# A hybrid decoder layer on one Trainium2 core: the second head's loads issued from ScalarE, and the first two pairs of channel blocks of the up projection interleaved

## The chip, the core and the metric

The kernel runs on one core of one Trainium2 chip. The metric is the device time of one execution in microseconds, lower is better. The engines are named as in the profile: PE (TensorE, matmuls; PEld its weight loads), DVE (VectorE), ACT (ScalarE), POOL (GpSimd) and SP (SyncE, which here issues DMAs). Each engine works its own instructions in program order; between engines there are semaphores.

## What is computed

One decoder layer over 2048 tokens with 1024 channels in float32: a mixer of three head groups (forgetting attention, mLSTM, HGRN2), and a gated feed-forward part with a causal convolution of three taps. Cut to what matters here:

```python
def _fox_attention(q, k, v, c):            # 8 heads of 64, causal, with forget gates c
    ...
        s = jnp.einsum('bhqd,bhkd->bhqk', qi, k) * scale
        s = s + ci[..., None] - c[:, :, None, :]
        ...
        p = jax.nn.softmax(s, axis=-1)
        return jnp.einsum('bhqk,bhkd->bhqd', p, v)

def _conv_glu(h, w_up, conv_w, conv_b, w_down):
    u = _causal_dwconv(h @ w_up, conv_w) + conv_b
    gate, up = jnp.split(u, 2, axis=-1)
    return (jax.nn.silu(gate) * up) @ w_down

def reference(x, ...):
    for l in range(DEPTH):                 # DEPTH = 1, D_MODEL = 1024, D_FF = 2816
        h = _rms(x, norm_mix_g[l])
        x = x + _mixer(h, ...)
        h = _rms(x, norm_ffn_g[l])
        x = x + _conv_glu(h, w_up[l], ffn_conv_w[l], ffn_conv_b[l], w_down[l])
    return x
```

## The kernel before

**Stages.** The input projection and the other mixers run to about 905 us of the profiled span, the attention from there to about 1378, the output projection to about 1585. Then comes the feed-forward part in two halves of 1024 tokens: up projection of half 0 to about 2017, down projection of half 0, then both again for half 1. Float32 products are made of three matmuls of operands split in a high and a low half (names with h and l, or w tiles in pairs): high by high, low by high, high by low.

**Attention** (`attention`, with its order written by hand). A head has four blocks of 512 queries, and a block `qb` has 4·qb + 4 steps `j` of 128 keys. A step makes scores `s` on PE (L936, L937, and a mask at L939), then on ACT the exponential `pf` (L943) and its high half `ph` (L945), then the low half `pl` on POOL or DVE (L949). Three steps later (SKEW) the products with V follow on PE (L962 to L964). The score tile in PSUM has two buffers. Between the scores PE also makes products for the row maxima of later blocks (L886), which DVE reduces; every finished block adds an `oT` on ACT (L970). A head's operands QA, KA, QB, KB and V lie in two sets of buffers, for even and odd heads, and come by ten DMAs (`att_load`, L851), all issued by SP. The second head's are called for in step 6 of the first head, right behind that step's scores; those of the other heads in the third step of the head before.

**Feed-forward, up** (`ffn_up`). The order of instructions here isn't written by hand: a scheduler with estimates of its own sets it when the kernel is built. The 22 pairs of channel blocks (`p`, a gate block and an up block each) are taken in the order 0, 11, 1, 12 and so on; each `p` is called a pair below: pair 1, pair 2 and so on in that order. For a pair the product of h and w_up is made by a Winograd scheme of seven block products rather than eight: b11, t4, b21, t2, t1, t3 and b22, each of 12 matmuls of 128x512 (L1339), named by the operand from h. The other operands are blocks of w_up or sums of them: a11, s2, a12, s1, s3, a22, s4 (`up_blocks`): four loads on SP (L1302), four sums on DVE (L1313), seven high halves on ACT (L1307) and as many low halves on POOL (L1308). For pair 1, a11, a12 and a22 are made early (`up_first`, L1288). The results lie in two PSUM tiles of 1024 columns (g and u), of four such tiles in all, so pair 3 writes the tiles of pair 1. DVE adds up partial results (L1383, L1389, L1390, L1393, L1395), then come the convolution (ACT L1353, DVE L1354 and L1355, and a halo on ACT, L1357), the gate (ACT L1398) and the product (DVE L1400). After every second pair the result's blocks and their sums are stored (`g_blocks`, ACT's DMAs, L1421 and L1428), and in half 0 the same is done for the weights of the down projection (`w_blocks`: SP's loads L1438, POOL's differences L1441, ACT's stores L1442).

The high and low halves of two of the operands from h, t3 and b22, don't exist before the output projection's buffers are free; they are made when the up projection of half 0 begins (`h_parts` with `h_split`: ACT L1227; DVE or POOL L1228; sums L1246).

## Time and profile before

| what | value |
|---|---|
| time, median of 3 runs | 2878.68 us (2875.48, 2878.68, 2880.37) |
| the profiled execution: its time | 2879.12 us |
| the profiled execution: its span | 2877.0 us |
| mean granted TensorE clock | 0.982 of full speed |
| matmuls, PE busy | 15053, 2788.7 us |
| DMA | 411.06 MB, 143 GB/s in the mean |

In the rows of the profile shown below, a timeline's row has the start in us from the span's start, the duration, the engine, the line, the operation, the tiles written and read and a count; in brackets stands idle time of the engine just before it, and what ended it. SPq and ACTq are the issues of DMAs, as the sequencer of SP or ACT spends time on them. A row of the chain of waits has the start, the duration and what the end of the program was waiting for then.

### The profile page before, as it was taken

To read this page: it belongs to the slowest core of one execution; us is meant where nothing else is said; L and a number is where in the kernel's file an instruction comes from. 1 tells how busy PE (TensorE), PEld (TensorE's weight loads), DVE (VectorE), ACT (ScalarE), POOL (GpSimd) and SP (SyncE) were. 2 spreads that over 40 slices of the span, in tenths; PEclk is the share of its full clock that TensorE was granted. 3 is DMA by queue.
4 is the path that set the end of the run, shared out by engine and by line. 5 is a ranking of instruction groups with operands and counts; after the bars stand their busy time and mean duration, and the time that the engine had idled before them with its cause. 6 is when DMAs were issued, how large, how long until landed. Compare 5 with 4: busy or idle time off the path is not lost. (4 is left out here: it accounts for less than half of the span.)

```text
span 2877.0 us, 42992 instructions
## 1 busy us (share of the span) xinstructions
PE 2788.7 (97%) x15053; PEld 2337.0 (81%) x15053; DVE 1938.7 (67%) x3523; ACT 1277.4 (44%) x2167; POOL 1481.5 (51%) x1451
## 2 busy tenths in 40 slices
PE   7999998999998999999999899999999999999999
PEld 7899996889997766776787688888788788888887
DVE  6336786264777787777446677776786677777655
ACT  4214322141322888888223444444454344434443
POOL 2346562344564678777001666665476445444443
PEclk9999997999998999999999999999999999999999
DMA  5424434333336534641456445545678333333766
GB/s 161 131 91 138 150 122 137 102 93 111 98 103 182 107 90 90 131 88 26 150 180 204 137 160 169 168 155 181 233 253 278 98 99 100 106 110 128 238 210 207
DMA packets 347160, 411.06 MB, mean 143 GB/s; under 512 B 47682, under 2 KB 234128, under 8 KB 344032
## 3 DMA queue, kind: packets, MB, share of 16 engines
q1 hardware_dynamic: 292560, 318.45, 37.3%
q10 hardware_dynamic: 51952, 81.45, 7.8%
q0 software_dynamic: 2432, 8.42, 0.8%
q8 instruction: 118, 1.93, 0.3%
q14 instruction: 98, 0.80, 0.1%
HBM read 280.24 MB, written 127.98 MB: 142 GB/s over the span
## 5 line engine op out<-in xcount | busy, mean ns | idle before, releaser
L1308 POOL TENSOR_TENSOR w<-w,w 128x512 fp32r<-128x512 f32 x302 | 403.2, 1349 | 404.6 <-ACT w L1307 349.4
L1496 PE MATMUL ps<-w,w 128*128 128x512 f32 x1848 | 423.3, 391 | 3.9 <-ACT w L1487 2.6
L1496 PEld LDWEIGHTS ps<-w,w 128*128 128x128 f32 x1848 | 348.2, 189 | 78.2 <-ACT w L1487 3.0
L215 PE MATMUL w<-whi,hhi 128*128 128x256 f32 (+1 forms) x1280 | 369.7, 289 | 2.7 <-DVE z L332 2.5
L215 PE MATMUL w<-wlo,hhi 128*128 128x256 f32 (+1 forms) x1280 | 370.2, 290 | 0.0
L215 PE MATMUL w<-whi,hlo 128*128 128x256 f32 (+1 forms) x1280 | 369.0, 288 | 0.0
L949 POOL TENSOR_TENSOR pl<-pf,ph 128x512 fp32r<-128x512 f32 (+2 forms) x240 | 288.4, 1218 | 110.1 <-ACT ph L945 73.7
L1489 POOL TENSOR_TENSOR w<-w,w 128x512 fp32r<-128x512 f32 x154 | 215.5, 1406 | 205.4 <-ACT w L1487 152.7
L1307 ACT ACTIVATE w<-w 128x512 fp32r<-128x512 f32 x302 | 180.7, 628 | 258.4 <-POOL w L1308 87.1
L1488 DVE TENSOR_TENSOR w<-w,w 128x512 fp32r<-128x512 f32 x154 | 177.0, 1159 | 110.1 <-ACT w L1486 103.9
L215 PEld LDWEIGHTS w<-whi,hhi 128*128 128x128 f32 x1280 | 245.0, 191 | 5.1 <-DVE z L332 3.0
L215 PEld LDWEIGHTS w<-whi,hlo 128*128 128x128 f32 x1280 | 244.8, 191 | 1.6 <-issue 0.2
L215 PEld LDWEIGHTS w<-wlo,hhi 128*128 128x128 f32 x1280 | 245.2, 192 | 0.7
L198 POOL TENSOR_TENSOR wlo<-wraw,whi 128x256 fp32r<-128x256 f32 (+1 forms) x224 | 171.7, 804 | 107.0 <-ACT whi L195 79.8
L1313 DVE TENSOR_TENSOR w<-w,w 128x512 f32<-128x512 f32 x176 | 149.6, 869 | 80.9 <-DMA w<-in_w_up_dram 74.3
L943 ACT ACTIVATE pf<-s 128x512 f32<-128x512 f32 (+1 forms) x320 | 172.2, 538 | 70.4 <-PE s L937 22.3
L945 ACT ACTIVATE ph<-pf 128x512 fp32r<-128x512 f32 (+1 forms) x320 | 185.1, 579 | 10.2
L901 DVE TENSOR_REDUCE mx<-m 128x1 f32<-128x512 f32 x192 | 130.6, 685 | 64.5 <-PE m L886 61.8
L1354 DVE SCALAR_TENSOR_TENSOR u<-ps,fcol,u 128x1023 f32<-128x1023 f32 x88 | 108.9, 1278 | 95.2 <-ACT u L1353 95.2
L1487 ACT ACTIVATE w<-w 128x512 fp32r<-128x512 f32 x154 | 96.6, 628 | 111.2 <-PE ps L1496 87.7
L1486 ACT ACTIVATE w<-w 128x512 fp32r<-128x512 f32 x154 | 95.9, 623 | 92.7 <-POOL w L1489 44.4
L886 PE MATMUL m<-KB,QB 70*128 70x512 f32 (+2 forms) x320 | 129.9, 415 | 3.4 <-DVE mx L890 3.4
(387 smaller groups left out, 7034.8 us busy)
## 6 DMA issues: line engine op xcount, KB each, us to landing
w<-in_w_up_dram SPq DMA_DIRECT2D x182, 256.0 KB
w<-s_g SPq DMA_DIRECT2D x154, 256.0 KB
w<-in_w_down_dram SPq DMA_DIRECT2D x110, 256.0 KB
wraw<-in_w_in_dram SPq DMA_DIRECT2D x48, 512.0 KB
s_g<-u ACTq DMA_DIRECT2D x88, 256.0 KB
w<-s_w SPq DMA_DIRECT2D x88, 256.0 KB
s_g<-w ACTq DMA_DIRECT2D x66, 256.0 KB
x<-in_x_dram SPq DMA_DIRECT2D x32, 512.0 KB
```

Of the source, the lines that this page charges most:

```text
L198: nc.gpsimd.tensor_tensor(lo[:, q + i, :], raw[:, i, :], h[:, i, :].bitcast(F32), op=ALU.subtract)
L215: nc.tensor.matmul(out, lsl(lhs[a], i), rsl(rhs[b], i), start=(i == 0 and j == 0), stop=(i == n - 1 and j == 2))
L901: nc.vector.tensor_reduce(mx[:, i, kb : kb + 1], m[:, 0:n], axis=AX.X, op=ALU.max)
L943: nc.scalar.activation(pf[:, c0:], s[:, c0:], AF.Exp)
L945: nc.scalar.activation(ph[:, c0:], pf[:, c0:], AF.Copy)
L949: eng.tensor_tensor(pl[:, c0:], pf[:, c0:], ph[:, c0:].bitcast(F32), op=ALU.subtract)
L1307: nc.scalar.activation(h, t, AF.Copy)
L1308: nc.gpsimd.tensor_tensor(lo, t, h.bitcast(F32), op=ALU.subtract)
L1313: nc.vector.tensor_tensor(t, x, y, op=op)
L1488: nc.vector.tensor_tensor(gl, gr, gh.bitcast(F32), op=ALU.subtract)
L1489: nc.gpsimd.tensor_tensor(wl, wr, wh.bitcast(F32), op=ALU.subtract)
L1496: nc.tensor.matmul(tiles[tile], g[x][:, tile * P : (tile + 1) * P], w[y], start=j == 0 and c == 0, stop=j == nj - 1 and c == 2,)
```

## The change

Two edits, of which the second restructures a loop. The lines of the changed kernel are 3 higher behind `att_load`, and 8 to 17 higher in and behind `ffn_up`.

```diff
--- before.py
+++ after.py
@@ -847,8 +847,11 @@
     V = k.t(k.pat[f"V{n % 2}"], [P, 16, 130], F32R, tag="V")
     st.update(QA=QA, KA=KA, QB=QB, KB=KB, V=V, h=h, n=n)
 
+
+    q = k.nc.scalar if n == 1 else k.nc.sync
+
     def ld(dst, src):
-        k.nc.sync.dma_start(dst.bitcast(F32), src)
+        q.dma_start(dst.bitcast(F32), src)
 
     ld(QB[0:64], k.s_qh[r])
     ld(KB[0:64], k.s_kh[r])
@@ -1320,10 +1323,15 @@
     s2 = sum_(s1, a11, ALU.subtract)
     s3 = sum_(a11, a21, ALU.subtract)
     s4 = sum_(a12, s2, ALU.subtract)
-    for n, t in (("a11", a11), ("s2", s2), ("a12", a12), ("s1", s1), ("s3", s3), ("a22", a22), ("s4", s4)):
-        if n in names:
-            blocks[n] = parts(t)
-    return blocks
+    made = [("a11", a11), ("s2", s2), ("a12", a12), ("s1", s1), ("s3", s3), ("a22", a22), ("s4", s4)]
+
+    def make(some):
+        for n, t in some:
+            if n in names:
+                blocks[n] = parts(t)
+
+    make(made[:4])
+    return blocks, lambda: make(made[4:])
 
 
 def ffn_up(k, hf, fw, first):
@@ -1361,36 +1369,35 @@
             nc.vector.scalar_tensor_tensor(u[:, 0:1], ha[:, 1:2], cw(1), u[:, 0:1], op0=ALU.mult, op1=ALU.add)
         return u
 
-    held = None
-    for p in (x for j in range(NP // 2) for x in (j, j + NP // 2)):
-        early = first if p == 0 else {}
-        w = up_blocks(k, fw, p, " ".join(n for n in ("a11", "s2", "a12", "s1", "s3", "a22", "s4") if n not in early))
+    def tmp():
+        return k.t(fw, [P, BLK], tag="tmp", bufs=4)
+
+    def channels(p, early):
+
+        names = " ".join(n for n in ("a11", "s2", "a12", "s1", "s3", "a22", "s4") if n not in early)
+        w, more = up_blocks(k, fw, p, names)
         w.update(early)
         g, u = ps_tile(k, [P, HALF]), ps_tile(k, [P, HALF])
         x, z, wd, y = g[:, :BLK], g[:, BLK:], u[:, :BLK], u[:, BLK:]
-
-        def tmp():
-            return k.t(fw, [P, BLK], tag="tmp", bufs=4)
-
         product(x, w["a11"], "b11")
-        p1 = tmp()
+        p1, u2 = tmp(), tmp()
         nc.scalar.activation(p1, x, AF.Copy)
         if early:
             product(wd, w["a22"], "t4")
             product(x, w["a12"], "b21", False)
         product(y, w["s2"], "t2")
-        u2 = tmp()
         nc.vector.tensor_tensor(u2, y, p1, op=ALU.add)
         if not early:
             product(x, w["a12"], "b21", False)
         product(z, w["s1"], "t1")
+        yield
+        more()
         product(y, w["s3"], "t3", False)
-        u3 = tmp()
-        nc.vector.tensor_tensor(u3, y, p1, op=ALU.add)
-        nc.vector.tensor_tensor(y, z, u3, op=ALU.add)
+        nc.vector.tensor_tensor(p1, y, p1, op=ALU.add)
+        nc.vector.tensor_tensor(y, z, p1, op=ALU.add)
         if not early:
             product(wd, w["a22"], "t4")
-        nc.vector.tensor_tensor(wd, u3, wd, op=ALU.subtract)
+        nc.vector.tensor_tensor(wd, p1, wd, op=ALU.subtract)
         product(z, w["s4"], "b22", False)
         nc.vector.tensor_tensor(z, z, u2, op=ALU.add)
 
@@ -1398,13 +1405,23 @@
         nc.scalar.activation(ug, ug, AF.Silu)
         uu = conv(u, NP + p)
         nc.vector.tensor_tensor(uu, ug, uu, op=ALU.mult)
-        if p < NP // 2:
-            held = uu
+        held.append(uu)
+
+    held, begun = [], []
+    for i, p in enumerate(x for j in range(NP // 2) for x in (j, j + NP // 2)):
+        begun.append(channels(p, first if p == 0 else {}))
+        next(begun[-1])
+        if hf == 0 and i == 0:
+
+            continue
+        while begun:
+            next(begun.pop(0), None)
+        if len(held) < 2:
             continue
         j = p - NP // 2
         if hf == 0:
             w_blocks(k, j)
-        g_blocks(k, hf, j, held, uu)
+        g_blocks(k, hf, j, held.pop(0), held.pop(0))
 
 
 def ps_tile(k, shape):
```

**The loads.** For the second head (n == 1) the ten DMAs are issued by ACT rather than SP. The order of ACT's instructions there, first before and then in the changed kernel, from step 6 of the first head on (pf and ph of a step have the lines L943 and L945, in the changed kernel L946 and L948):

```order
L943 ACTIVATE pf_10119<-s_10116 128x512
L945 ACTIVATE ph_10121<-pf_10119 128x512
L943 ACTIVATE pf_10153<-s_10150 128x512
L945 ACTIVATE ph_10155<-pf_10153 128x512
L970 ACTIVATE oT_10168<-pv_10073 65x512
```

```order
L948 ACTIVATE ph_10121<-pf_10119 128x512
L854 DMA QB_10137<-s_qh 64x2048
L854 DMA KB_10138<-s_kh 64x2048
L854 DMA QB_10137<-s_one 6x2048
L854 DMA KB_10138<-s_one 4x2048
L854 DMA KB_10138<-s_fc 2x2048
L854 DMA QA_10135<-s_qh 64x2048
L854 DMA QA_10135<-s_ql 64x2048
L854 DMA KA_10136<-s_kl 64x2048
L854 DMA KA_10136<-s_kh 64x2048
L854 DMA V_10139<-s_v 128x16x130
L946 ACTIVATE pf_10153<-s_10150 128x512
```

The ten stand between ph of step 6 and pf of step 7. On SP, where they stood between the first head's last parts and the third head's loads, nothing takes their place. The DMAs issued by SP and ACT use eight semaphores in turn, in the program's order over both; each waits until the DMA eight places back has landed.

**The pairs.** A pair is now a generator (`channels`) with a stop behind t1. In half 0 pair 1 goes to that stop, then pair 2 goes to it, and then both are finished; all later pairs run through at once, as before. `up_blocks` makes the operands of the first four products first, and those of t3, t4 and b22 behind the stop. A pair's temporaries are two rather than three. Behind pair 2 the pairs' instructions and their order are the same, with other buffers.

What PE runs is the same set of matmuls. Before, pair 1's t3 and b22 come before most of pair 2; in the changed kernel the order from pair 1's t1 on is: b11 x2 and t2 x2 of pair 2, t3 x2 of pair 1, then b11 x10, t2 x10, b21 x12 and t1 x12 of pair 2, t3 x10 of pair 1, t3 x12 of pair 2, b22 of pair 1, t4 and b22 of pair 2, b11 of pair 3.

POOL's order there, from the first low halves of pair 1 (s2 and s1) on. Before (L1308 makes low halves of operands from w_up, L1228 those of b22, L1441 the differences for the down projection; the fifth L1308 row is a11 of pair 2):

```order
L1308 TENSOR_TENSOR w_17883<-w_17876,w_17882 128x512
L1308 TENSOR_TENSOR w_17887<-w_17874,w_17886 128x512
L1308 TENSOR_TENSOR w_17891<-w_17878,w_17890 128x512
L1308 TENSOR_TENSOR w_17895<-w_17880,w_17894 128x512
L1228 TENSOR_TENSOR b22l<-w_17828,b22h 128x512
L1228 TENSOR_TENSOR b22l<-w_17838,b22h 128x512
L1228 TENSOR_TENSOR b22l<-w_17848,b22h 128x512
L1228 TENSOR_TENSOR b22l<-w_17858,b22h 128x512
L1441 TENSOR_TENSOR w_18164<-w_18157,w_18156 128x512
L1308 TENSOR_TENSOR w_18022<-w_18005,w_18021 128x512
L1308 TENSOR_TENSOR w_18026<-w_18015,w_18025 128x512
```

And in the changed kernel (L1308, L1228 and L1441 are now L1311, L1231 and L1458):

```order
L1311 TENSOR_TENSOR w_17883<-w_17876,w_17882 128x512
L1311 TENSOR_TENSOR w_17887<-w_17874,w_17886 128x512
L1231 TENSOR_TENSOR b22l<-w_17828,b22h 128x512
L1231 TENSOR_TENSOR b22l<-w_17838,b22h 128x512
L1231 TENSOR_TENSOR b22l<-w_17848,b22h 128x512
L1458 TENSOR_TENSOR w_18162<-w_18155,w_18154 128x512
L1231 TENSOR_TENSOR b22l<-w_17858,b22h 128x512
L1311 TENSOR_TENSOR w_17973<-w_17956,w_17972 128x512
L1311 TENSOR_TENSOR w_17977<-w_17966,w_17976 128x512
L1458 TENSOR_TENSOR w_18163<-w_18157,w_18162 128x512
L1311 TENSOR_TENSOR w_17981<-w_17962,w_17980 128x512
L1458 TENSOR_TENSOR w_18164<-w_18157,w_18155 128x512
```

Two of pair 1's low halves (s3 and s4) no longer stand there, so pair 2's a11 (w_17973) is the eighth rather than the tenth; its s2 (w_17977), a12 (w_17981) and s1 follow, with differences for the down projection between them, and pair 1's s3 and s4 behind those.

DVE's order behind pair 2's temporary u2, in the changed kernel (L1316 makes sums of w_up blocks, old L1313; L1396, L1397, L1400 and L1402 are the old L1389, L1390, L1393 and L1395; L1362 is the convolution's old L1354; tmp_17904 and ps_17890 and 17891 belong to pair 1, ps_17988 and 17989 to pair 2):

```order
L1389 TENSOR_TENSOR tmp_18003<-ps_17989,tmp_18002 128x512
L1316 TENSOR_TENSOR w_18196<-w_18190,w_18192 128x512
L1316 TENSOR_TENSOR w_18198<-w_18196,w_18188 128x512
L1316 TENSOR_TENSOR w_18200<-w_18188,w_18190 128x512
L1316 TENSOR_TENSOR w_18202<-w_18194,w_18198 128x512
L1396 TENSOR_TENSOR tmp_17904<-ps_17891,tmp_17904 128x512
L1397 TENSOR_TENSOR ps_17891<-ps_17890,tmp_17904 128x512
L1400 TENSOR_TENSOR ps_17891<-tmp_17904,ps_17891 128x512
L1396 TENSOR_TENSOR tmp_18002<-ps_17989,tmp_18002 128x512
L1397 TENSOR_TENSOR ps_17989<-ps_17988,tmp_18002 128x512
L1402 TENSOR_TENSOR ps_17890<-ps_17890,tmp_17905 128x512
L1362 SCALAR_TENSOR_TENSOR u_18078<-ps_17890,fcol,u_18078 128x1023
```

Ahead of pair 1's L1396 now stand the four sums of pair 3's blocks (w_18196 to w_18202), which read w_up tiles (w_18188 to w_18194) that SP loads. Before, four sums of pair 2 stood ahead of it. A sum of pair 4 (w_18346) follows two rows behind the last one shown, ahead of the convolution's further operations for pair 1.

In the output projection the scheduler also orders some transposes, splits and loads of the second to fourth tile of 128 tokens differently; no instruction is added or removed there.

## The prediction

> **What bounds the kernel now.** I read the page's head first, then the chain of waits around the two places of the change, then the timelines of single engines there.
>
> ```profile
> span 2877.0 us, 42992 instructions
> PE 2788.7 (97%) x15053; PEld 2337.0 (81%) x15053; DVE 1938.7 (67%) x3523; ACT 1277.4 (44%) x2167; POOL 1481.5 (51%) x1451
> ```
>
> PE is busy for 97% of the span, so the time is PE's work plus PE's holes, and no matmul is added or removed. An edit pays only if it closes a hole of PE and costs only if it opens one. The two places look quite different in the table of stretches (columns: stretch, its length, busy time of PE, PEld, DVE, ACT and POOL with counts, granted clock, DMA share, GB/s):
>
> ```profile
> 938.00:945.00 7.00, 7.00 (x37) 5.16 (x37) 5.98 (x14) 5.71 (x11) 4.90 (x4) 1.00 1.02 218
> 945.00:950.00 5.00, 5.00 (x30) 3.70 (x29) 4.26 (x10) 3.14 (x8) 2.46 (x3) 1.00 1.09 208
> 1594.00:1600.00 6.00, 5.33 (x25) 3.85 (x24) 4.93 (x6) 4.32 (x9) 5.17 (x4) 1.00 0.73 231
> 1600.00:1610.00 10.00, 5.64 (x20) 3.07 (x18) 10.00 (x7) 3.64 (x7) 10.00 (x7) 1.00 0.62 183
> 1610.00:1621.00 11.00, 7.39 (x18) 5.38 (x19) 6.08 (x7) 3.45 (x6) 11.00 (x9) 0.53 0.23 72
> 1620.00:1800.00 180.00, 180.00 (x794) 148.72 (x794) 129.33 (x148) 79.11 (x125) 114.29 (x86) 1.00 0.46 149
> ```
>
> Where the loads of the second head now stand in ScalarE's order (941 us), PE has **no hole at all**: there is nothing to win there and everything to lose. At the start of the up projection PE has a hole of (6 - 5.33) + (10 - 5.64) + (11 - 7.39) = 8.6 us, and much of the last stretch ran at about half clock; from 1620 on it is full again. The hole is all that the second part of the change can win.
>
> **Part 1: ten loads on ScalarE's queue.** What one head's loads take of the engine that issues them is seen for the third head, whose loads find their buffers free:
>
> ```profile
> 985.46 0.45 SPq L851 DMA_DIRECT2D QB<-s_qh  x1
> 985.95 0.60 SPq L851 DMA_DIRECT2D KB<-s_kh  x1
> ...
> 988.94 0.60 SPq L851 DMA_DIRECT2D KA<-s_kl  x1
> 990.75 0.45 SPq L851 DMA_DIRECT2D KA<-s_kh  x1
> 993.85 0.39 SPq L851 DMA_DIRECT2D V<-s_v  x1
> ```
>
> Eight issues go out in 4.1 us; then the ninth stands until 990.75 and the tenth until 993.85. The program signals such transfers on eight semaphores in turn, so the ninth waits for the landing of the first (QB) and the tenth for that of the second (KB). From first to last that is 994.24 - 985.46 = **8.8 us** of the issuing engine. SP has nothing else to do. ScalarE does, and the ten now stand between two of its steps:
>
> ```profile
> 940.65 0.63 ACT L945 ACTIVATE ph<-pf 128x512 fp32r<-128x512 f32 x1
> 941.27 0.60 ACT L943 ACTIVATE pf<-s 128x512 f32<-128x512 f32 x1
> 941.90 0.63 ACT L945 ACTIVATE ph<-pf 128x512 fp32r<-128x512 f32 x1
> 942.44 0.58 ACT L970 ACTIVATE oT<-pv 65x512 f32<-65x512 f32 x1
> 942.91 0.60 ACT L943 ACTIVATE pf<-s 128x512 f32<-128x512 f32 x1
> ...
> 942.12 0.39 PE L936 MATMUL s<-QB,KB 70*128 70x512 f32 x1
> ...
> 943.89 0.42 PE L936 MATMUL s<-QB,KB 70*128 70x384 f32 x1
> ```
>
> The first ph above is that of step 6; the ten loads come behind it, and the pf of step 7 (941.27) behind them. If ScalarE is held from 941.3 for 8.8 us, that pf ends at 950.1 + 0.6 = 950.7. The score tile has two buffers: PE starts the scores of step 8 at 942.12, but those of step 9 (943.89) need the buffer that the pf of step 7 empties. So PE stops at 943.89 and goes on at about 950.75: a hole of **6.9 us**. Behind the stopped scores on PE stand the maxima and the products with V of all later steps, so VectorE and GpSimd run dry too and can work nothing ahead. ScalarE has no slack to win it back: a step takes it 0.60 + 0.63 = 1.23 us, and PE goes from 942.12 to 943.89 for a step and its extras. So the hole shifts everything behind it.
>
> That a ScalarE step waits behind an issue that itself waits is shown by before's own stores there. Of those that read or write s_g the trace lists the engines that waited for them:
>
> ```profile
> ACT tmp L1377: 32.7, 7
> ```
>
> Seven operations of ScalarE with no operand in s_g waited 32.7 us, because they stand behind such stores in its queue.
>
> On top comes the clock. The stretch 1610 to 1621 followed a stop of PE and has 0.53. The matmuls there show what it costs:
>
> ```profile
> 1614.83 0.79 PE L1339 MATMUL ps<-b22h,w 128*128 128x512 f32 x1 [2.80 <-DVE ps L1390]
> ...
> 1615.84 1.05 PE L1339 MATMUL ps<-b22h,w 128*128 128x512 f32 x2
> 1616.70 0.63 PE L1339 MATMUL ps<-b22l,w 128*128 128x512 f32 x1
> ...
> 1620.93 0.61 PE L1339 MATMUL ps<-b11h,w 128*128 128x512 f32 x2
> 1621.38 0.39 PE L1339 MATMUL ps<-b11l,w 128*128 128x512 f32 x1
> ```
>
> Two matmuls take 1616.70 - 1615.84 = 0.86 us there and 1621.38 - 1620.93 = 0.45 us later. About 4 us at half clock after the new hole lose 2 us. The Trainium skill says the same of it (TensorE: Matmul & The Clock Gate, Part 1): the clock halves after an idle window of about 3.4 us and comes back after a busy one; the 0.53 beside the hole above agrees.
>
> The bounds of part 1. Upward: 6.9 us and a slow stretch of 10 us as in 1610 to 1621, which loses 5, in all +12 to +13. Downward: if the last two issues hardly waited, ten issues at the 0.25 to 0.60 us of the third head's rows are about 5 us, pf of step 7 ends at 946.9 and PE waits 3.0 us. Below nothing: the old loads were issued earlier, and one stop of PE lies among them:
>
> ```profile
> 919.90 0.91 SPq L851 DMA_DIRECT2D QB<-s_qh  x1
> ...
> 937.60 0.39 SPq L851 DMA_DIRECT2D V<-s_v  x1
> ...
> 931.06 0.58 PE L936 MATMUL s<-QB,KB 70*128 70x256 f32 x1 [4.01 <-ACT pf L943]
> ```
>
> If their traffic delayed what ends this stop, up to 4 us could come back. I count none of it: these loads queue on SP behind the first head's own parts, so what runs before 931 is mostly the first head's. SP itself, freed of the loads, has nothing behind them until 985.46. I take 6.9 + 2 = **+9**, bounds -4 and +13, nearest to the third head's row.
>
> The Trainium skill has a rule that speaks against this part (DMA: Bandwidth & Descriptors, Issuing engines are not separate DMA queues): transfers from all issuers run on the same 16 engines, and another issuer saves only the sequencer's time to issue. By the rows SP lacked no such time, which agrees, so the rule leaves the part without a gain.
>
> **Part 2: the first two pairs together.** The chain of waits through the hole:
>
> ```profile
> 1600.21 4.02 DVE t3l L1228 x3
> ...
> 1604.96 1.76 DVE w L1313
> ...
> 1608.31 5.12 DVE w L1313 x3
> 1613.44 0.61 DVE tmp L1389
> ...
> 1614.07 0.71 DVE ps L1390
> ...
> 1614.83 178.90 PE ps L1339 x776
> ```
>
> Before, PE waits for VectorE's t3l, and then for the sums of the second pair that stand on VectorE ahead of L1389 and L1390. The change lets the second pair's products run ahead of t3, so those sums no longer stand before a result that PE lacks. But their **inputs are not ready sooner**. GpSimd is the late engine then:
>
> ```profile
> 1594.83 6.27 POOL L1308 TENSOR_TENSOR w<-w,w 128x512 fp32r<-128x512 f32 x4 [57.46 <-ACT w L1307]
> 1601.06 6.78 POOL L1228 TENSOR_TENSOR b22l<-w,b22h 128x512 fp32r<-128x512 f32 x4
> 1607.80 1.73 POOL L1441 TENSOR_TENSOR w<-w,w 128x512 f32<-128x512 f32 x1
> 1609.50 5.07 POOL L1308 TENSOR_TENSOR w<-w,w 128x512 fp32r<-128x512 f32 x3
> ```
>
> It works without a break from 1594.83. The new order takes two of the first four (3.1 us, to 1598), then four b22l and one L1458 (the old L1441), 8.5 us from about 1601, when b22h is there, to 1609.5. Only then comes the low half of the second pair's a11, the third matmul's operand: about 1611. PE has by then finished t1 of the first pair (1601.0), and does only two b11, two t2 and two t3, 1.4 us of work in 10 us. I walk on at 1.7 us for each operation of GpSimd while VectorE is busy too: a12's low half (behind s2's and one L1458) at 1615.7, s1's (behind another L1458) at 1618.3. PE's half clock lasts to about 1617; t1 of the second pair ends at about 1623.8, the 22 remaining t3 at 1628.8. That is the 72nd matmul behind the first pair's t1. Before, the 73rd (the third pair's first) starts here:
>
> ```profile
> 1630.22 0.39 PE L1339 MATMUL ps<-b11h,w 128*128 128x512 f32 x1
> ```
>
> So up to here the new order wins **1.4 us** of the 8.6. Then b22 of the first pair is due, and needs the new L1397. On VectorE that stands behind four sums of the third pair, which wait for loads; SP can issue the fourth of these only when GpSimd has done the first pair's s3, about 1620. A load of this kind stands in the chain of waits with 3.4 to 5.8 us elsewhere:
>
> ```profile
> 1901.43 5.79 DMA w<-in_w_up_dram
> ...
> 2236.83 3.40 DMA w<-in_w_up_dram
> ```
>
> With the other waits on GpSimd in these sums, L1397 ends between 1628.6 and 1632; I take 1630.4, so b22 starts level with before (a stop of 1.6). Behind it stand b22 of pair 1, t4 and b22 of pair 2: 36 matmuls, 8.2 us, to 1638.6. In this time VectorE must run the whole convolution of pair 1 to free the PSUM tile that the third pair's b11 writes. The conv's parts by their rows:
>
> ```profile
> 1621.08 1.21 ACT L1353 ACTIVATE u<-ps,fcol 128x1024 f32<-128x1024 f32 x1 [6.92 <-DVE ps L1395]
> 1622.33 1.28 DVE L1354 SCALAR_TENSOR_TENSOR u<-ps,fcol,u 128x1023 f32<-128x1023 f32 x1 [1.28 <-ACT u L1353]
> ```
>
> From the end of pair 1's b22 (1633.1): 0.7 for L1402, 1.2 for ScalarE, 1.3 for L1362 (to 1636.3), 0.7 for L1400 of pair 2, then **a sum of the fourth pair in between that waits for loads** (L1316; 1638.5 to 1641), 1.3 for the other L1362, 1.3 for L1363: about 1642. PE stops for 3.4 us, and 0.6 more at t2. Sum of part 2: -1.4 + 1.6 + 3.4 + 0.6 = **+4**. Bounds: -9, if the whole hole closes, and +7, if both loads land at the late ends.
>
> The same loop's first tiles also change the order of some transposes and loads in the output projection (1378 to 1400). No instruction is added there and the few stops of PE are under 1 us each: 0, bounds -1 and +1.
>
> **The sum.** The profiled execution took 2879.12 us, close to the median of 2878.68. 2879.1 + 9 + 4 = 2892; as some of the late 2 us may lie under the next pair's work, **2891**.
>
> **The rivals.** (a) *ScalarE isn't held*: the issues slip in at under 0.4 us each and the waits are short (the 3.0 us above) or the old traffic did cost the stop at 931 (-4), and part 2 wins 6 to 8 of its hole: 2879 - 2 - 7, about **2870**. Against it: the third head's 8.8 us. (b) *Part 2 closes the hole, and pays for part 1*: the one mechanism is that GpSimd has the second pair's a11 low before PE ends t1 (1601 to 1604), so that 48 matmuls of the second pair cover VectorE's t3l. Its price is -9 at most; from -3.2 on (9 - 3.2 = 5.8) the kernel is not slower beyond what can be told: about **2880**. Against it: four b22l stand ahead in GpSimd's order. (c) *Longer slow clock behind the stop at 944*, and late loads in part 2: 2879 + 13 + 7, about **2899**. (d) *The change does less than it says*: with transfers as the limit, the issuer wouldn't matter; part 2 alone: 2879 + 4 = **2883**. The skill's rule above would give this one, if ScalarE's issues cost as little as it says.
>
> **How the numbers follow.** Forecast (2886 to 2896) 0.47; (c) 0.15; (d) 0.11; (b) 0.13; (a) 0.14. A measurement of this kernel can tell about 0.2% or 5.8 us from no change, so slower means above 2884.5 and faster below 2872.9. Slower: 0.47 + 0.15 + 0.02 of (d) = 0.64; within: 0.09 of (d), 0.10 of (b) and 0.03 of (a), 0.22; faster: 0.14. The range takes in (b), (c) and (d) and the upper half of (a): 2869 to 2903.
>
> **What would show it.** Step by step: ten issues on ScalarE's queue between 941 and 950, the last two apart from the others; scores on PE (L939) idle 6 to 7 us at 944, then a clock of 0.5 for 3 to 7 us. In the up projection: PE idle 8 us around 1601 to 1611 (shifted by part 1), released by GpSimd's L1311; b22 of pair 1 waiting for L1397; the third pair's b11 waiting for the conv. Wrong if PE runs on at 944, or if the first t2 products of the second pair run through without a stop.

## The result, and the profile after

| kernel | median of its runs | ratio to the kernel before | 95% interval |
|---|---|---|---|
| changed kernel, first comparison (4 runs; before 2878.25 us, 4 runs) | 2900.06 us | 1.0064 | 1.0052 to 1.0077 |
| the same again, beside other kernels (5 runs; before 2881.66 us, 21 runs) | 2893.38 us | 1.0049 | 1.0036 to 1.0061 |

The change makes the kernel **slower by about half a per cent**, 12 to 22 us. The profiled execution of the changed kernel took 2895.74 us against 2879.12 us before, so 16.6 us more. The head of its page:

```profile
span 2893.9 us, 42982 instructions
PE 2789.8 (96%) x15053; PEld 2336.1 (81%) x15053; DVE 1941.7 (67%) x3523; ACT 1276.0 (44%) x2167; POOL 1484.4 (51%) x1451
```

PE's busy time is the same within 1.1 us (2788.7 before), while the span grew by 16.9 us. That doesn't make all of it holes: matmuls at a slow clock count as busy for longer, and there are more of these at the places of the change and fewer elsewhere. To see where the time goes I take the same matmul of both traces by its number in PE's order and compare the starts:

```
matmul   before     changed   difference   where
  6001    882.53     885.38      +2.9      before anything of the change
  6401    959.01     969.37     +10.4      attention, 20 us behind the loads
  8401   1352.41    1362.45     +10.0      attention, last head
  9201   1519.87    1529.07      +9.2      output projection
  9565   1600.03    1608.10      +8.1      up projection, pair 1's t1
 10401   1802.39    1820.94     +18.6      up projection, nine pairs on
 14801   2813.20    2830.13     +16.9      last down projection
```

So the time goes at two places: **7.5 us at the loads** (10.4 - 2.9) and **10.5 us at the start of the up projection** (18.6 - 8.1). The first 2.9 us are not the change's: PE runs the same matmuls in the same order up to there, and other executions differ as much (last section). At the loads PE stands still for 5.15 us and is busy for 2.6 us more; from pair 1's t1 on, over 600 matmuls, it stands still for 5.9 us more than before and is busy for 4.6 us more, by the slow clock.

At the loads, the timeline of ScalarE in the changed kernel:

```profile
943.29 0.63 ACT L948 ACTIVATE ph<-pf 128x512 fp32r<-128x512 f32 x1
943.30 0.50 ACTq L854 DMA_DIRECT2D QB<-s_qh  x1
943.84 0.60 ACTq L854 DMA_DIRECT2D KB<-s_kh  x1
...
946.99 0.61 ACTq L854 DMA_DIRECT2D KA<-s_kl  x1
948.15 0.45 ACTq L854 DMA_DIRECT2D KA<-s_kh  x1
950.80 0.39 ACTq L854 DMA_DIRECT2D V<-s_v  x1
951.29 0.60 ACT L946 ACTIVATE pf<-s 128x512 f32<-128x512 f32 x1 [7.36 <-DMA KB<-s_kh]
```

and that of PE:

```profile
946.52 0.27 PE L916 MATMUL m<-ident,m 128*4 128x128 f32 x1
951.94 0.69 PE L939 MATMUL s<-QB,KB 70*128 70x384 f32 x1 [5.15 <-ACT pf L946]
```

The ten loads stand between ph of step 6 and pf of step 7; the ninth waits until 948.15, the tenth until 950.80, for landings of QB and KB (the bracket of pf names KB's). Only then comes pf, and PE's scores have stood for it for 5.15 us.

The table of stretches of the changed kernel (columns as in the prediction):

```profile
952.00:960.00 8.00, 8.00 (x33) 5.72 (x34) 3.91 (x8) 5.14 (x11) 2.97 (x3) 0.69 1.00 213
1600.00:1612.00 12.00, 8.24 (x38) 5.95 (x36) 9.64 (x10) 6.91 (x13) 6.88 (x5) 1.00 0.91 282
1612.00:1620.00 8.00, 4.95 (x10) 2.54 (x11) 8.00 (x6) 3.97 (x7) 8.00 (x5) 0.52 0.18 65
1620.00:1636.00 16.00, 15.86 (x64) 12.40 (x62) 7.70 (x6) 3.36 (x6) 16.00 (x13) 0.92 0.35 113
1636.00:1656.00 20.00, 14.07 (x53) 10.78 (x53) 15.97 (x20) 10.94 (x16) 11.15 (x8) 0.91 0.22 67
1656.00:1684.00 28.00, 28.00 (x125) 23.16 (x124) 18.91 (x19) 8.23 (x15) 19.00 (x14) 1.00 0.50 169
1684.00:1692.00 8.00, 6.00 (x20) 4.46 (x19) 7.07 (x7) 3.34 (x8) 3.75 (x3) 0.79 0.49 142
```

Behind the stop at 946 the clock is 0.69 for 8 us. In the up projection the old hole (8.6 us before) is still there, (12 - 8.24) + (8 - 4.95) = 6.8 us, now between 1600 and 1620. Two new ones stand behind it: 5.9 us between 1636 and 1656, and 2.0 us between 1684 and 1692. PE's timeline names them, with the releaser in brackets:

```profile
1637.57 0.50 PE L1347 MATMUL ps<-b22h,w 128*128 128x512 f32 x1 [1.50 <-DVE ps L1397]
...
1649.41 0.50 PE L1347 MATMUL ps<-b11h,w 128*128 128x512 f32 x1 [3.39 <-ACT halo L1365]
...
1655.07 0.50 PE L1347 MATMUL ps<-t2h,w 128*128 128x512 f32 x1 [1.04 <-ACT halo L1365]
...
1687.31 0.70 PE L1347 MATMUL ps<-b11h,w 128*128 128x512 f32 x1 [2.00 <-ACT halo L1365]
```

They are pair 1's b22, waiting for L1397; pair 3's b11 and t2, waiting for the convolutions of pair 1's two PSUM tiles to empty them; and pair 5's b11, waiting for the convolution of pair 3. VectorE's timeline shows what held pair 3's b11:

```profile
1642.60 1.28 DVE L1362 SCALAR_TENSOR_TENSOR u<-ps,fcol,u 128x1023 f32<-128x1023 f32 x1 [1.28 <-ACT u L1361]
1643.80 0.68 DVE L1400 TENSOR_TENSOR ps<-tmp,ps 128x512 f32<-128x512 f32 x1
1646.08 0.69 DVE L1316 TENSOR_TENSOR w<-w,w 128x512 f32<-128x512 f32 x1 [1.59 <-DMA w<-in_w_up_dram]
1646.69 1.28 DVE L1362 SCALAR_TENSOR_TENSOR u<-ps,fcol,u 128x1023 f32<-128x1023 f32 x1
1647.88 1.27 DVE L1363 SCALAR_TENSOR_TENSOR u<-ps,fcol,u 128x1022 f32<-128x1022 f32 x1
```

A sum of pair 4's blocks (L1316 at 1646.08) stands in the middle of pair 1's convolution and waits for its load.

### The profile page after: what moved, and what is told of

It reads as the page before. It is cut to its first block, busy times and chain, and to the rows that moved or that the text cites. A ratio compares the mean times of both kernels' runs of the same rounds, so it can differ in the third digit from the quotient of the medians.

```text
span 2893.9 us, 42982 instructions
## 1 busy us (share of the span) xinstructions
PE 2789.8 (96%) x15053; PEld 2336.1 (81%) x15053; DVE 1941.7 (67%) x3523; ACT 1276.0 (44%) x2167; POOL 1484.4 (51%) x1451
## 5 line engine op out<-in xcount | busy, mean ns | idle before, releaser
L1311 POOL TENSOR_TENSOR w<-w,w 128x512 fp32r<-128x512 f32 x302 | 406.2, 1357 | 402.0 <-ACT w L1310 343.0
L1310 ACT ACTIVATE w<-w 128x512 fp32r<-128x512 f32 x302 | 180.0, 627 | 270.2 <-POOL w L1311 85.1
L1316 DVE TENSOR_TENSOR w<-w,w 128x512 f32<-128x512 f32 x176 | 154.3, 895 | 88.7 <-DMA w<-in_w_up_dram 75.6
L946 ACT ACTIVATE pf<-s 128x512 f32<-128x512 f32 (+1 forms) x320 | 172.1, 538 | 76.7 <-PE s L940 22.2
L948 ACT ACTIVATE ph<-pf 128x512 fp32r<-128x512 f32 (+1 forms) x320 | 185.2, 579 | 10.3
L1362 DVE SCALAR_TENSOR_TENSOR u<-ps,fcol,u 128x1023 f32<-128x1023 f32 x88 | 108.9, 1279 | 92.4 <-ACT u L1361 92.4
```

The costliest lines, as they stand in the source:

```text
L946: nc.scalar.activation(pf[:, c0:], s[:, c0:], AF.Exp)
L948: nc.scalar.activation(ph[:, c0:], pf[:, c0:], AF.Copy)
L1310: nc.scalar.activation(h, t, AF.Copy)
L1311: nc.gpsimd.tensor_tensor(lo, t, h.bitcast(F32), op=ALU.subtract)
L1316: nc.vector.tensor_tensor(t, x, y, op=op)
```

## The experiments

Two theories were to be tested, one for each part. For the loads: ScalarE is held by the issues that wait for a landing. Rivals: the number of issues costs, or the loads' later transfer. For the pairs: VectorE's and SP's orders hold the third and fifth pair. Rivals: GpSimd is the limit, or a lateness that moves on from pair to pair, whatever order is mended. The kernels were run in four groups, each beside the kernel before on one chip. Besides the ratio I give the cost at its own place, from the trace of each: the time from the 6291st to the 6401st matmul of PE for the loads (21.0 us in the kernel before), and the time from the last matmul of pair 1's t1 to the 600th behind it for the pairs (148.9 us).

| kernel | median us (before) | ratio, 95% interval | loads: us | pairs: us |
|---|---|---|---|---|
| before | | | 21.0 | 148.9 |
| changed, first profile | 2900.06 (2878.25) | 1.0064, 1.0052 to 1.0077 | 28.8 | 159.4 |
| whole (changed again) | 2893.38 (2881.66) | 1.0049, 1.0036 to 1.0061 | 28.7 | 157.2 |
| a_only | 2886.60 (2880.91) | 1.0015, 1.0005 to 1.0025 | 28.9 | 148.9 |
| b_only | 2890.85 (2880.91) | 1.0030, 1.0019 to 1.0041 | 21.0 | 159.7 |
| a_eight | 2883.94 (2880.91) | 1.0009, 0.9999 to 1.0019 | 22.9 | 148.3 |
| a_spread | 2880.30 (2880.91) | 0.9991, 0.9981 to 1.0001 | 21.1 | 148.9 |
| b_w1 | 2890.63 (2881.66) | 1.0033, 1.0020 to 1.0046 | 21.3 | 155.7 |
| b_w01 | 2887.50 (2881.66) | 1.0021, 1.0012 to 1.0031 | 21.0 | 152.9 |
| w_next | 2881.87 (2881.66) | 0.9999, 0.9987 to 1.0010 | 21.0 | 146.1 |
| b_conv | 2893.12 (2879.31) | 1.0045, 1.0031 to 1.0060 | 21.3 | 158.4 |
| b_w01_conv | 2885.72 (2879.31) | 1.0027, 1.0016 to 1.0038 | 21.1 | 153.0 |
| sums_w | 2880.26 (2879.31) | 1.0000, 0.9991 to 1.0010 | 21.0 | 147.5 |
| b_conv_w1 | 2892.50 (2882.54) | 1.0031, 1.0019 to 1.0042 | 21.0 | 159.8 |

**Each part alone.** a_only is the kernel before with the first hunk of the change, b_only the changed kernel with `q = k.nc.sync`.

> The first part alone: the second head's ten loads on ScalarE's queue, the up projection as before. Theory: the whole cost of this part is one stop of PE while ScalarE is held, so the shift of PE against before is the 7.5 us that the changed kernel shows between 917 and 969 us, and nothing later gives it back: about 2878 + 7.5 = 2885.5. Rival 1: the cost comes only together with the second part (a shifted schedule of clock windows or of loads in the up projection), then this kernel is within 3 us of before. Rival 2: the loads' later transfer delays the third head's too, then more stops of PE stand behind 969 us and the time is over 2890.

> The second part alone: the first two pairs together, all loads on SP's queue. Theory: the stops of PE at the third pair's first product (3.6 us and the slow clock behind it) and at the fifth pair's (2.2 us and the slow clock) come back at the same places, and it costs 9 to 10 us: about 2888. Rival 1: the recorded schedule of the up projection is only slow because the first part shifted it; then it is within 3 us of before or faster. The two parts' costs should add up to the 21.8 us of the whole change within 5 us; if they don't, something of the whole is in neither.

> The changed kernel as it is, beside the kernel before on the same chip as the others. Theory: the parts add up, 2880.9 + 5.7 + 9.9 = 2896.5 by the first four runs' medians; with the first comparison's 21.8 us it would be 2902. Over 2900 would mean that something of the whole is in neither part.

The parts act at their own places only: a_only has the stop at the loads (28.9 us) and the old up projection (148.9), b_only the reverse. In ratios, 0.15% and 0.30% make 0.45%, against 0.49% of the whole in the next group and 0.64% in the first comparison; the last lies above the sum, but its interval (0.52 to 0.77) and the sum's (about 0.30 to 0.60, from the two intervals added in squares) overlap. In the traces it is 7.9 and 10.8 us for the parts at their places, and 7.7 and 10.5 or 7.7 and 8.3 for the two profiles of the whole. So neither part hides or worsens the other as far as this can be told, and rival 1 of both fell.

How much a place can tell is seen here too. Three executions of the same interleaved pairs (changed, whole, b_only) have 159.4, 157.2 and 159.7 us, and four of the old order (before, a_only, a_eight, a_spread) 148.3 to 148.9. So below, a difference of 2.5 us between single traces of interleaved pairs shows nothing; what is read from them is the stops themselves.

**The loads: eight on ScalarE, two on SP.**

```diff
         ld(QA[64:128, c], k.s_ql[r, c])
         ld(KA[0:64, c], k.s_kl[r, c])
+        q = k.nc.sync
         ld(KA[64:128, c], k.s_kh[r, c])
         ld(V[:, j0:j1], v[:, j0:j1])
+        q = k.nc.scalar if n == 1 else k.nc.sync
```

> As the first part alone, but the last two of the ten loads (KA's high part and V, the two that wait for an earlier load's landing) stay on SP. Theory: ScalarE is held only for the eight issues, 4.3 us rather than 8.0, so pf of step 7 ends 1.5 us later than PE needs it rather than 5.2, and the cost is about 2 us: 2880. Rival 1: what costs is the issuing itself, in proportion to the number: eight tenths of 7.5 us, 2884. Rival 2: it is the loads' later transfer, whoever issues them: 2885.5 as with all ten.

**The loads: one a step.** The loads are issued by the same generator, which now stops behind each:

```diff
     for dst, src in (
...
     ):
         ld(dst, src)
+        if n == 1:
+            yield
...
-                            for _ in att_load(k, h + 1, sts[h + 1]):
-                                pass
+                            slow = att_load(k, h + 1, sts[h + 1])
+                            for _ in slow:
+                                if h == 0:
+                                    break
+                        elif h == 0 and slow is not None:
+                            next(slow, None)
```

> All ten loads on ScalarE's queue, but one in each of ten steps of the attention (steps 6 to 15) rather than all between two steps. Theory: nothing waits for a landing, since each is issued over 1 us after the one before; ScalarE only loses the issue time of 0.3 to 0.6 us a step, 4.5 us in all, and some of this lies in the idle time of 0.3 to 2.3 us that it has in steps with masks: no stop of PE over 1 us, cost 0 to 3 us, about 2879.5. Rival 1: the cost is that of ten issues on a busy ScalarE wherever they stand: 4.5 us or more, 2883. Rival 2: the cost is that of the loads coming late: 2885 or more, as they come later still.

With eight, ScalarE is free again when the last issue is out, and PE's stop is as expected. ScalarE in a_eight, and then PE, from their timelines:

```profile
947.84 0.61 ACTq L853 DMA_DIRECT2D KA<-s_kl  x1
948.55 0.60 ACT L947 ACTIVATE pf<-s 128x512 f32<-128x512 f32 x1 [3.77 <-DMA QB<-s_qh]
```

```profile
949.20 0.44 PE L940 MATMUL s<-QB,KB 70*128 70x384 f32 x1 [1.56 <-ACT pf L947]
```

The cost at the place falls from 7.9 to 1.9 us. Two of ten issues carry three quarters of it, so it isn't the number of issues (6 us would have stayed), and not the later transfer. The medians alone (3.0 us more than before, interval -0.3 to 5.5) would not rule out rival 1. Spread over ten steps the loads cost nothing that the place shows (21.1 against 21.0 us), less than I expected at most. Why is seen in ScalarE's rows of a_spread:

```profile
941.64 0.60 ACT L956 ACTIVATE pf<-s 128x512 f32<-128x512 f32 x1
942.27 0.64 ACT L958 ACTIVATE ph<-pf 128x512 fp32r<-128x512 f32 x1
942.27 0.50 ACTq L853 DMA_DIRECT2D QB<-s_qh  x1
942.88 0.60 ACT L956 ACTIVATE pf<-s 128x512 f32<-128x512 f32 x1
```

The issue (ACTq) runs from 942.27 to 942.77, beside ph, and the next pf starts at 942.88, no later than without it. One issue of up to 0.6 us behind an operation of 0.64 us is covered; ten in a row are not, and a wait in the queue is not.

**The pairs: SP's order at pair 5.** In b_w1 the second set of down-projection weights is called for later:

```diff
         next(begun[-1])
+        if hf == 0 and i == 4:
+            w_blocks(k, 1)
         if hf == 0 and i == 0:
...
-        if hf == 0:
+        if hf == 0 and j != 1:
             w_blocks(k, j)
```

> The second part alone, but the second set of down-projection weights (w_blocks for j = 1) is called for behind the start of pair 5 rather than ahead of it. This moves only those: SP's four loads of pair 5 stand together again, ahead of the four loads of w_down, as in the kernel before; the start of the up projection is the same. Theory: the stop of PE at pair 5's first product (2.2 us, and some 2 us of slow clock behind it) comes from SP's order, two loads of pair 5 queued behind four that wait for buffers of the first stores; so it goes and the time falls by 4 us to about 2887. Rival: VectorE is late there anyway, from the third pair's stop on; then the stop stays and the time is that of the second part alone, 2891.

**The pairs: GpSimd freed.** In b_w01 it is `i in (2, 4)` with `w_blocks(k, i // 2 - 1)`, and `j > 1` below.

> As the kernel before this one, and the first set (j = 0) is called for behind the start of pair 3, so that GpSimd has none of its differences ahead of the second and third pairs' low halves, and SP's loads of w_down stand behind pair 4's. Theory: GpSimd is the late engine in the hole: freed of 1.7 us ahead of a11's low half of pair 2 and of 4.7 us ahead of pair 1's s3, the products b21 and t1 of pair 2 and the loads of pair 3 come 2 to 5 us sooner, the stops at b22 of pair 1 and at pair 3's first product shrink from 7 us (with their slow clock) to 0 to 3; time 2877 to 2883, level with before. Rival: VectorE's order (sums of pairs 3 and 4 ahead of pair 1's results) is the limit, whatever GpSimd does: the stops stay and the time is 2886 to 2887.

In b_w1 PE has no stop at pair 5; the table of stretches has, where the changed kernel and b_only stop:

```profile
1650.00:1700.00 50.00, 50.00 (x217) 41.25 (x217) 34.63 (x37) 19.83 (x33) 25.23 (x20) 0.98 0.28 91
```

That is what the theory says; the place's cost falls from 10.8 to 6.8 us, by the 4 us expected. The medians don't show it (0.33% against 0.30% for b_only, with intervals of 0.26% and 0.22%), so the time of this step rests on the trace alone. The later call moves not only SP's loads but also GpSimd's differences and ScalarE's stores of that set, which this run doesn't tell apart from SP's order. How SP came to be late there is read in the changed kernel's timeline and chain of waits:

```profile
1663.35 0.98 SPq L1305 DMA_DIRECT2D w<-in_w_up_dram  x2
1664.38 5.04 SPq L1455 DMA_DIRECT2D w<-in_w_down_dram  x4
1670.86 0.93 SPq L1305 DMA_DIRECT2D w<-in_w_up_dram  x2
```

```profile
1665.69 5.09 DMA s_g<-u
1670.78 0.02 issue
1670.80 0.03 SPq L1305
1670.83 0.03 issue
1670.86 5.05 DMA w<-in_w_up_dram
1675.93 1.23 DVE w L1316
```

Two of pair 5's loads are issued, then four of w_down, then the other two; before, all four of pair 5 stood ahead of w_down's. The third load goes out only when the store s_g of the first results has landed, because in the program that store is eight DMAs back and shares the load's semaphore. It is the same sharing that holds the ninth and tenth load in the attention.

In b_w01 the first theory and its rival are both half right. The products up to pair 2's b22 gained: the stop at b22 is gone and pair 2's last t3 comes 4.1 us sooner, counted from t1, than in the kernel before (24.96 against 29.06 us for the 72nd matmul behind t1; it is 26.63 in b_w1, so 1.7 us are this step's). But the stop at pair 3's b11 grew and took this back (PE's timeline of b_w01, then VectorE's):

```profile
1645.55 0.80 PE L1347 MATMUL ps<-b11h,w 128*128 128x512 f32 x1 [6.05 <-ACT halo L1365]
```

```profile
1639.23 0.69 DVE L1316 TENSOR_TENSOR w<-w,w 128x512 f32<-128x512 f32 x1 [4.43 <-DMA w<-in_w_up_dram]
```

VectorE waits 4.43 us with pair 4's sum at the head of its queue, the convolution of pair 1 behind it.

**The pairs: VectorE's order.** In b_conv an order-only edge puts pair 4's sums behind pair 1's convolution:

```diff
-        w, more = up_blocks(k, fw, p, names)
+        if hf == 0 and p == 1 + NP // 2:
+            with k.tc.issue_after(conved[1].ins):
+                w, more = up_blocks(k, fw, p, names)
+        else:
+            w, more = up_blocks(k, fw, p, names)
```

where `conved` holds the convolutions' last operations. b_w01_conv has the same in b_w01, b_conv_w1 in b_w1.

> The second part alone, with one order more: on VectorE the four sums of pair 4's blocks are queued behind the convolution of pair 1 (in the second part alone the first of them stands in the middle of it, and waits for a load). Theory: the stop of PE at pair 3's first product comes from that one place, so it shrinks from 3.5 us (and its slow clock, some 6 us together) to the 1 us or less that the convolution's own operations need behind b22; pair 5's stop stays. 2885 to 2887. Rival: the convolution's own chain (VectorE's two and ScalarE's operations) is as long as the cover of 24 matmuls, and the stop stays at 2 us or more: 2889 to 2891.

> As the kernel before this one, and with both sets of down-projection weights called for later, as in the kernel b_w01. Theory: with GpSimd freed there was a gain of 4 us up to b22 of pair 2, all taken back by the wait of VectorE for pair 4's load (PE's stop grew to 6.2 us); without that wait the gain is kept, and pair 5's stop is gone too: 2 to 5 us faster than before, 2876 to 2880. Rival: pair 4's sums, now behind the convolution, make pair 4's own products late, and the stop moves there: 2884 or more.

> The second part alone with both orders of the runs b_conv and b_w1: pair 4's sums behind pair 1's convolution on VectorE, and the second set of down-projection weights called for behind the start of pair 5, so that SP's four loads of pair 5 stand together ahead of them. Theory: the two stops have two places, and each order takes away its own: at pair 3's first product 1.3 us stay (1.8 more at its t2), at pair 5's none, as in b_w1. From pair 2's t1 to pair 6 PE then loses 3 to 4 us against the kernel before rather than 9 to 11: 2882 to 2884. Rival: lateness once begun moves on from pair to pair through VectorE's sums, whichever order is mended: a stop of 2 us or more stands at pair 5 again and the time is 2888 or more.

In b_conv the stop at pair 3's b11 shrank as forecast (1.60 us more stand at its t2), and that at pair 5 grew (PE's timeline):

```profile
1643.57 0.50 PE L1347 MATMUL ps<-b11h,w 128*128 128x512 f32 x1 [1.09 <-ACT halo L1367]
...
1682.41 0.79 PE L1347 MATMUL ps<-b11h,w 128*128 128x512 f32 x1 [3.97 <-ACT halo L1367]
```

so pair 4's sum was what held pair 3's b11 (2.81 us in b_only, 3.39 in the changed kernel), but most of the time won is lost at pair 5, where b_only stops for 2.39 us, and the median is no better than b_only's (1.0045 against 1.0030). b_w01_conv shows the same, 3.59 us more than a matmul's usual distance ahead of pair 5's b11, and no gain over b_w01 (153.0 against 152.9 us). In b_conv_w1, where both orders are mended, pair 5's first product waits again, this time through ScalarE, whose part of the convolution comes late behind high halves that wait for GpSimd (L1311); and two stops of 1 us follow at 1698 and 1718. PE's and VectorE's timelines:

```profile
1676.38 0.80 PE L1347 MATMUL ps<-b11h,w 128*128 128x512 f32 x1 [2.99 <-ACT halo L1367]
```

```profile
1672.46 2.47 DVE L1362 SCALAR_TENSOR_TENSOR u<-ps,fcol,u 128x1023 f32<-128x1023 f32 x2 [3.77 <-ACT u L1361]
```

My forecast for this run fell, and its rival, a lateness that moves on from pair to pair whichever order is mended, seems to stand. But **the edge changed more than VectorE's order**, and this the theory and the rival both left out: the scheduler set PE's order anew. What PE runs behind the last matmul of pair 3's b22, in b_only and then in b_conv:

```profile
1670.40 0.39 PE L1347 MATMUL ps<-b22h,w 128*128 128x512 f32 x1
1670.63 0.39 PE L1347 MATMUL ps<-b21h,w 128*128 128x512 f32 x1
...
1681.34 0.80 PE L1347 MATMUL ps<-b11h,w 128*128 128x512 f32 x1 [2.39 <-ACT halo L1365]
```

```profile
1672.61 0.39 PE L1347 MATMUL ps<-b22h,w 128*128 128x512 f32 x1
1672.83 0.39 PE L1347 MATMUL ps<-t1h,w 128*128 128x512 f32 x1
```

In b_only pair 4's b21, t1 and t3 lie between pair 3's b22 and pair 5's b11: 36 matmuls, 8.2 us, under which pair 3's convolution can run. In the three kernels with the edge b21 comes ahead of pair 3's t4 and b22, and 24 matmuls are left, 2.7 us less. In b_conv the way from that last b22 to pair 5's b11 is even 1.1 us shorter than in b_only (9.8 against 10.9 us); the stop is longer because the cover is shorter. In b_conv_w1 it is 8.8 us, so an estimate from these numbers is that 0.4 us of its 2.99 us would have stayed with 36 matmuls. Ahead of pairs 6 and 7 it has the shorter cover again, with a stop each; ahead of pair 8 there are 36 matmuls and no stop. So **these runs don't show that lateness moves on by itself**, nor do they test two separate places: no run has the edge with PE's old order. In b_w1, where PE's order is b_only's, the stop at pair 5 went and none came behind it.

The lowest cost of the interleaved pairs is b_w01's, 4.0 us after 10.8; of this, b_w1's later call alone gave 4.0, and calling the first set later, which frees GpSimd but moves SP's loads and ScalarE's stores too, 2.8 more.

**The kernel before, improved the same way.** w_next calls for the first set of down-projection weights in pair 3, with the old order of the pairs; sums_w adds an edge that puts pair 2's sums behind pair 1's L1390.

```diff
         product(z, w["s1"], "t1")
+        if hf == 0 and i == 2:
+            w_blocks(k, 0)
         product(y, w["s3"], "t3", False)
...
-        if hf == 0:
+        if hf == 0 and j > 0:
             w_blocks(k, j)
```

> The kernel before, with one change: the first set of down-projection weights is called for in pair 3 rather than in pair 2. Neither part of the change is in it. Theory: GpSimd's difference between b22's low halves and pair 2's a11 goes (1.7 us), so the stop at pair 2's first t2 products shrinks by 1 to 1.5 us, and little else: VectorE sets the other stops. 1 to 3 us faster than before, which 5 rounds may not tell. Rival: GpSimd sets more of the hole by slowing VectorE's sums (1.7 us rather than 0.7 while both run); then the hole loses 4 us or more.

> The kernel before (neither part of the change), with two orders changed: VectorE's four sums of pair 2 behind pair 1's L1390, on which b22 waits, and the first set of down-projection weights called for in pair 3. Theory: of the 8.6 us hole of PE in the kernel before, the stop of 2.8 us ahead of b22 and the longest wait for t3l (2.4 us) come from sums standing ahead on VectorE, so they go, with most of the slow clock; pair 2's s2 comes later and a stop of 1 to 2 us stands at its t2 products instead. 3 to 6 us faster than before. Rival: GpSimd is the limit for all of pair 2 and what is won ahead of b22 is lost at t2 and b21: within 1.5 us of before.

The hole of the kernel before shrank in both, by 2.7 us in w_next and, for the first 264 matmuls behind t1, by 4.6 us in sums_w (67.93 against 72.58 us), of which 3.3 us were lost again at later pairs. Neither is faster than the kernel before within what the runs tell (0.9999 and 1.0000, intervals of 0.23% and 0.19%). None of the kernels tried is shown to beat it; a_spread comes nearest, and its interval includes 1.

## Why the prediction was right, and where it was not

The forecast was 2891 us (2886 to 2896), slower by 12 us, in a range of 2869 to 2903; measured were 12 to 22 us more than before. The 2893 us of the second comparison lie close to it partly by luck: part 1 was put 1.3 us too high and part 2 6.5 us too low. The 2900 us of the first lie nearest to rival (c)'s 2899, of which one half came: the loads of part 2 were late, but the slow clock behind the stop at the loads cost 2.5 us and not 5.

- **The base.** PE sets the time and no matmul goes: right. The 16.9 us are stops of PE and the slow clock behind them.
- **ScalarE held for 8.8 us.** Right in mechanism (a_eight, a_spread), a little high in size: from the first issue at 943.30 to the end of the last at 951.19 it is 7.9 us, as both landings come a little sooner (the ninth issue 4.85 us behind the first, for 5.29 at the third head), and the first issue lies beside ph. PE's stop is 5.15 us for 6.9 forecast, and with the slow clock behind it (0.69 for 8 us, so 2.5 us) the place costs 7.7 us for the 9 forecast. Rival (a), ScalarE not held, and rival (d), the issuer not mattering, fell. The rule of the Trainium skill (DMA: Bandwidth & Descriptors, Issuing engines are not separate DMA queues) holds in what it says of the gain, none here; of what the new issuer loses it says nothing. Of the old traffic's delay of the stop at 931 (up to -4) little is seen: that stop is 4.01 us before, 3.98 in the changed kernel and 3.57 in a_spread, which issues the loads later still. One reading was wrong: ScalarE does have slack, 1.23 us of work in PE's 1.77 us a step by the prediction's own rows, and a_spread's issues fit into it. What can't be won back is PE's lost time.
- **The hole at the start of the up projection.** Forecast: GpSimd is the late engine, the hole stays, and 1.4 us are won by pair 2's last t3. Measured 2.4 us (26.67 against 29.06 us for the 72nd matmul). Most of the hole's stops, 5.8 of 6.8 us, name ScalarE's high halves (L1310) rather than GpSimd as forecast; but the last one, behind which PE's run goes on, waits for GpSimd's low half of pair 2's a11, at the time forecast (1611, and this kernel is 8 us later there). PE, then GpSimd:

```profile
1612.04 0.55 PE L1347 MATMUL ps<-b11h,w 128*128 128x512 f32 x1 [2.65 <-ACT w L1310]
...
1618.47 0.80 PE L1347 MATMUL ps<-b11h,w 128*128 128x512 f32 x1 [0.56 <-POOL w L1311]
```

```profile
1616.71 3.40 POOL L1311 TENSOR_TENSOR w<-w,w 128x512 fp32r<-128x512 f32 x2
```

b_w01 agrees with GpSimd's part (1.7 us), without separating it. Rival (b), the hole closed, fell.

- **b22 of pair 1 waits for L1397:** 1.6 us forecast, 1.50 measured. **Pair 3's b11 waits for the convolution:** 3.4 forecast, 3.39 measured, by the step named (pair 4's sum in the middle of it, shown by b_conv). **Its t2:** 0.6 forecast, 1.04 measured; but with the same pairs it is 0.35 in whole and 2.64 in b_only, and b11's stop 3.51 and 2.81, so the match to a tenth is chance.
- **What was missing.** The sum of part 2 is 10.5 us, 4 were forecast. The sum ended at pair 3's t2, and the later pairs were put at nothing: in the part on the change they stand as the same in instructions and order. They weren't: SP's loads of pair 5 were parted, and one waits for a late store. That is 2.0 us and the slow clock behind it (0.79 for 8 us, 1.7 us), together 3.7. And no slow clock was counted behind pair 3's stop: 0.91 for 20 us, about 1.8 us. These 5.5 us are most of the 6.5 missing. The forecast of part 1 had such a term; that of part 2 did not. In whole the same stop at pair 5 has no slow clock behind it (1.00, where the changed kernel has 0.79), which is most of the 2.2 us between the two profiles there:

```profile
1684.00:1692.00 8.00, 6.54 (x29) 5.42 (x30) 6.65 (x9) 2.69 (x6) 3.25 (x4) 1.00 0.56 166
```

- **Given back.** 2.3 us come back between the loads and the up projection (10.4 at the 6401st matmul, 8.1 at the 9565th), where the prediction put 0, and 1.6 us behind the up projection of half 0 (18.6 at the 10401st, 16.9 at the 14801st). No run tells why; over the first of these stretches a_only, with the old output projection, is 2.1 us longer than the kernel before, so single executions differ by as much.

**Left open:** whether the stops of the interleaved pairs can all be mended, since no run mended VectorE's order with PE's kept as it was. What b_w1 and b_w01 owe to SP, to GpSimd and to ScalarE is not told apart either. More buffers for the blocks of w_up, which would let loads start sooner, were not tried.

## What to carry to other kernels

A transfer may be issued from a busy compute engine where one issue lies beside one operation; ten in a row, or one that must wait for an earlier landing, hold that engine's whole queue, so count the waits of each issue and not its bytes. When two units of work are interleaved, follow the order of every queue until PE runs full again, loads and shared semaphores too, not only to the end of the units; and count a slow clock behind each stop of PE as likely, though not as certain. Where a scheduler sets the order, an edge meant for one queue can change the others: compare the order of every engine before reading what such a run shows, and look at the sum over the following units before calling it a gain.

## What the runs showed of the hardware that was not expected

- ScalarE's sequencer issues a DMA while ScalarE still executes the operation ahead of it: in a_spread both start at 942.27, the issue takes 0.50 us and the operation 0.64, and the next operation starts at 942.88.
- The slow clock doesn't follow every stop. At PE's stop at pair 5 the granted clock is 0.5 for 3.41 us in the changed kernel and in b_only (stops of 2.00 and 2.39 us) and for 6.83 us in b_conv (3.97 us); in whole (1.83 us) it stays at 1.00.
- Executions differ where the code does not. The 6001st matmul, ahead of all that was changed, starts at 882.53 us in the kernel before, at 881.29 in a_only, 885.38 in the changed kernel and 888.40 in w_next. The spread of 7 us is more than any single step here costs apart from the two parts, which is why such steps were read from the traces at their own place, and why medians of 5 to 12 runs leave intervals of 0.2%.
